# A two-layer encoder on one core: rotary keys as column tiles in the input stage, one product for both meta values, and a new order on TensorE

## The chip, the cores and the metric

The kernel runs on one core of one Trainium2 chip. The metric is the device time of the whole program in microseconds (us), lower is better. TensorE (PE) multiplies matrices into the banks of PSUM; VectorE (DVE), ScalarE (ACT) and GpSimd (POOL) work element by element; SyncE (SP) issues transfers (DMA).

## What is computed

Two request groups, one of 256 tokens and one of 512, each with 16 meta tokens ahead, pass through the same two layers, in float32. 272 + 528 = 800 tokens in all. Cut to what matters:

```python
for i in range(2):
    mix = mla_mixer(h, ...) if i == 0 else gqa_mixer(h, ...)
    h = layer_norm(DN_ALPHA * h + mix, ln1_g[i], ln1_b[i])
    h = layer_norm(DN_ALPHA * h + sqrelu_mlp(h, w1, w2), ln2_g[i], ln2_b[i])
return h[:, N_META:]

def mla_mixer(x, ...):                       # dense attention, 16 heads
    c = x @ w_in                             # 1024 -> 768 (q) + 256 (kv) + 32 (rotary key)
    cq, ckv = rms_norm(c[..., :768], g_q), rms_norm(c[..., 768:1024], g_kv)
    kr = apply_rope(c[..., 1024:], cos, sin) # one rotary key for all heads
    q = cq @ w_uq                            # per head 64 plain + 32 rotated
    kn, v = split(ckv @ w_ukv)
    s = qn @ kn + qr @ kr                    # softmax(s / sqrt(96)) @ v, then @ w_o

def gqa_mixer(x, ...):                       # window of 128, 16 query heads, 4 key heads, sinks
    q, k, v = split(x @ w_qkv)               # meta tokens are seen by every block

def sqrelu_mlp(x, w1, w2):
    h = relu(x @ w1)
    return (h * h) @ w2
```

## The kernel before

Activations lie with features on the 128 partitions and tokens along the free axis, in halves of 400 columns. For accuracy every large product is three products of fp32r operands: an operand is split into a rounded high part and the remainder, and `mm3` adds high x high, high x low and low x high in one bank (lines 510, 511 and 512 of the profile). The splits cost one ACT cast and one DVE subtraction each.

*Input stage.* `c = x @ w_in` is computed in columns of 128 features, in the order `IN_ORDER = [6, 7, 8, 0, 1, 2, 3]`, and columns 4 and 5 at the end by `pair`, which saves products by sums of blocks (a Strassen-like scheme). Columns 6 and 7 are ckv, column 8 is the rotary key, repeated four times to fill 128 features, columns 0 to 5 are cq. Weights of the first three columns and the eight slices of x come in quarters and slices from SP's queue; PE works through three columns as slices land. `post` evicts a column: for column 8 four DVE operations make the rotated key `kr` from two tables; for others it stores the column and adds its squares up on DVE. After column 8 `key_norm` takes the root of the mean of squares of ckv: `rstd_bcast` splits the sums, lets PE add them over partitions and broadcast them in one go, and takes Sqrt on ACT and the reciprocal on DVE over 128 x 400 elements. `sums(k)` makes the block sums for `pair` from x, for which slices are loaded again (`load_again`) save those kept in their buffers (`KEPT`).

*Planned stages.* From attention on, each stage is a list of tasks given to `Plan.task` with engine, cost in ns, what it reads and writes. `Plan.order` simulates the stage by these costs and writes the instructions down in the order of their simulated begins. The order on PE isn't left to it: `ORDERS` holds a permutation of PE's tasks for each of four stages (attention of layer 0, its MLP, attention of layer 1, its MLP). Costs decide the order on the other engines, and for tasks given by `either` whether POOL or DVE does them (the weight sums of the MLP's Strassen-like products, for instance, line 1502). `Plan.lag` is the time from the end of a task to the start of one that waits for it.

*Attention of layer 0.* Scores go to two banks `sa`; a group of scores is one chunk of queries for one pair of heads or one head. DVE takes the negative maximum (line 1124), ACT the exponential (line 1128 or 1138), then a reciprocal and a scaling, PE transposes the probabilities (`wa<-ident,p`, line 1186) and multiplies them with the values as fp32 products in two column tiles of 64 (`wa<-pt,v`, line 1219). An fp32 product shows as two records.

*Attention of layer 1.* `values` computes v in blocks of 128 tokens, and apart from them the 16 meta tokens of each group as a product of 16 rows.

Of the kernel before, what the change touches and what calls it, by code (L numbers as in the profile page):

```python
# [47 lines left out]
IN_ORDER = [6, 7, 8, 0, 1, 2, 3]  # L48
# [3 lines left out]
KEPT = (3,)  # L52
# [78 lines left out]
]  # L131


LEAD = (1400, 3000, 1400, 0)


class Held:


    def __init__(self, tag, make, t=None):  # L140
        self.tag, self.make, self.t, self.left, self.fresh, self.after = tag, make, t, 0, True, ()


class Plan:

    LAG = {"PE": 190, "DVE": 70, "ACT": 70, "POOL": 90, "SP": 0}

    last, count = {}, 0

    def __init__(self, bufs, own, in_turn=()):
        self.bufs, self.own, self.tasks, self.last, self.ways = bufs, own, [], {}, []
        self.no, Plan.count = Plan.count, Plan.count + 1
# [2510 lines left out]
```

## Time and profile before

| | |
|---|---|
| median of 3 runs | 1743.28 us (1742.0 to 1743.66) |
| the profiled execution | 1743.47 us, span 1741.6 us |
| granted clock of TensorE, mean | 0.998 |
| PE busy | 1726.0 us, 99% of the span, 10806 records |
| DVE busy | 1432.8 us, 82% |
| ACT busy | 1027.5 us, 59% |
| POOL busy | 335.4 us, 19% |
| DMA | 124.15 MB, mean 71 GB/s |

Busy times are from records; records of one engine overlap their neighbours, so a share near 100% doesn't yet say that no time is left between two instructions. The distance from start to start tells more.

### The profile page before, as it was taken

What the parts mean: (1) busy time and instruction counts of PE and PEld (TensorE: products, weight loads), DVE (VectorE), ACT (ScalarE), POOL (GpSimd) and SP (SyncE); (2) the same over time, 40 slices, a digit from 0 to 9 for tenths busy, and PEclk for the clock granted to TensorE, in tenths of its full rate; (3) what the DMA queues carried; (4) which work ended last, traced back from release to release, by engine and by line L of the source; (5) the groups of instructions that cost most, each with busy time, mean ns of one, the idle gap of its engine ahead of it and who ended that gap; (6) DMA issues with size and microseconds to landing.
All of it is one profiled execution on the core that took longest, in us unless ns stands there. A gap on an engine that the chain in (4) does not pass through costs nothing.

```text
span 1741.6 us, 28738 instructions
## 1 busy us (share of the span) xinstructions
PE 1726.0 (99%) x10806; PEld 1628.5 (94%) x10806; DVE 1432.8 (82%) x2921; ACT 1027.5 (59%) x2172; POOL 335.4 (19%) x306
## 2 busy tenths in 40 slices
PE   9999999999999999999999999999999999999998
PEld 9999999989999999999999998889989889988996
DVE  7888888887877899888886887876877889889877
ACT  6577777774755446445644627775665455545652
POOL 0011111112210111111202223332201133322200
PEclk9999999999999999999999999999999999999999
DMA  7201001014311221122122221012311222222222
GB/s 253 78 32 32 20 23 54 23 42 164 99 61 49 73 67 67 61 85 73 52 75 99 88 85 57 26 50 76 106 61 49 73 74 73 73 73 73 73 68 90
DMA packets 39451, 124.15 MB, mean 71 GB/s; under 512 B 4752, under 2 KB 9744, under 8 KB 39184
## 3 DMA queue, kind: packets, MB, share of 16 engines
q1 hardware_dynamic: 39312, 122.31, 21.2%
q8 instruction: 85, 1.39, 0.3%
q14 instruction: 54, 0.44, 0.1%
HBM read 119.15 MB, written 3.15 MB: 70 GB/s over the span
## 4 chain that ended last, share of the span: by engine, by line
PE 97%; DVE 2%; ACT 1%; issue 0%; DVEq 0%; POOL 0%; ACTq 0%; POOLq 0%
PE w L510 18%; PE w L511 18%; PE w L512 18%; PE wb L510 4%; PE wb L511 4%; PE wb L512 4%; PE wa L510 3%; PE wa L512 3%; PE wa L511 3%; PE wa L1219 2%; PE sa L510 2%; PE wa L1186 2%; PE sa L512 2%; PE sa L511 2%; PE wb L2373 2%; PE wb L2355 2%
## 5 line engine op out<-in xcount | busy, mean ns | idle before, releaser
L1798 DVE TENSOR_TENSOR acc<-acc,w 128x400 f32<-128x400 f32 (+1 forms) x306 | 183.5, 620 | 53.7 <-PE w L512 51.4
L510 PE MATMUL w<-h,wspi 128*128 128x400 f32 x320 | 110.2, 344 | 0.8 <-DVE acc L1305 0.8
L511 PE MATMUL w<-h,wspi 128*128 128x400 f32 x320 | 110.3, 345 | 0.0
L512 PE MATMUL w<-h,wspi 128*128 128x400 f32 x320 | 110.2, 344 | 0.0
L510 PE MATMUL w<-h,wsp 128*128 128x400 f32 x312 | 108.0, 346 | 0.4 <-DVE acc L1798 0.4
L511 PE MATMUL w<-h,wsp 128*128 128x400 f32 x312 | 107.7, 345 | 0.2 <-DVE h L1530 0.2
L512 PE MATMUL w<-h,wsp 128*128 128x400 f32 x312 | 107.3, 344 | 0.0
L1530 DVE TENSOR_TENSOR h<-sq,h 128x400 fp32r<-128x400 f32 (+1 forms) x167 | 102.2, 628 | 3.5 <-ACT h L1528 3.3
L1528 ACT CAST h<-sq 128x400 fp32r<-128x400 f32 (+1 forms) x167 | 84.3, 518 | 19.9 <-DVE sq L1536 10.9
L1155 POOL TENSOR_TENSOR p<-p,rs 106x512 f32<-106x512 f32 (+1 forms) x40 | 45.0, 1126 | 251.4 <-DVE pk L1146 117.6
L1128 ACT ACTIVATE p<-sa,nm,rq 106x528 f32<-106x528 f32 (+1 forms) x80 | 63.5, 794 | 17.0 <-DVE nm L1125 12.6
L1709 ACT COPY sq<-w 128x400 f32<-128x400 f32 (+1 forms) x69 | 33.6, 487 | 67.7 <-PE w L512 67.0
L1124 DVE TENSOR_REDUCE nm<-sa 106x1 f32<-106x528 f32 (+1 forms) x80 | 56.2, 704 | 16.2 <-PE sa L512 14.7
L510 PE MATMUL w<-wsp,h 128*128 128x512 f32 (+1 forms) x176 | 69.5, 395 | 0.0
L512 PE MATMUL w<-wsp,h 128*128 128x512 f32 (+1 forms) x176 | 69.2, 393 | 0.0
L512 PE MATMUL w<-wspi,h 128*128 128x512 f32 (+1 forms) x176 | 69.1, 393 | 0.0
L510 PE MATMUL w<-wspi,h 128*128 128x512 f32 (+1 forms) x176 | 69.1, 392 | 0.0
L511 PE MATMUL w<-wspi,h 128*128 128x512 f32 (+1 forms) x176 | 69.1, 392 | 0.0
L511 PE MATMUL w<-wsp,h 128*128 128x512 f32 (+1 forms) x176 | 69.1, 392 | 0.0
L510 PE MATMUL sa<-k,q 128*106 128x264 f32 (+5 forms) x208 | 64.0, 308 | 2.9 <-ACT p L1138 2.9
L510 PE MATMUL w<-t,wspi 128*128 128x400 f32 (+1 forms) x180 | 61.5, 342 | 0.0
L512 PE MATMUL w<-t,wspi 128*128 128x400 f32 (+1 forms) x180 | 61.5, 342 | 0.0
(824 smaller groups left out, 6173.1 us busy)
## 6 DMA issues: line engine op xcount, KB each, us to landing
wrawo<-in_w_o_dram SPq DMA_DIRECT2D x32, 512.0 KB, 3.3
wraw0d<-in_w2b_dram SPq DMA_DIRECT2D x24, 512.0 KB, 3.3
wraw1d<-in_w2b_dram SPq DMA_DIRECT2D x18, 512.0 KB, 3.5
wrawq<-in_w_q_dram SPq DMA_DIRECT2D x8, 512.0 KB, 3.3
xr<-in_xT_dram SPq DMA_DIRECT2D x16, 200.0 KB, 3.1
wraw<-in_w_qn_dram SPq DMA_DIRECT2D x8, 384.0 KB, 3.0
wx1d<-in_w2b_dram SPq DMA_DIRECT2D x6, 512.0 KB, 3.3
out_dram<-fo SPq DMA_DIRECT2D x11, 256.0 KB, 2.0
```

What stands on the lines that cost most here:

```text
L510: nc.tensor.matmul(out, lh, rh, start=start, stop=False, **kw)
L511: nc.tensor.matmul(out, lh, rl, start=False, stop=False, **kw)
L512: nc.tensor.matmul(out, ll, rh, start=False, stop=stop, **kw)
L1124: plan.task("DVE", DVE(528), lambda: V.tensor_reduce(nm.t[:qm, 0:1], v(), axis=AX.XY, op=ALU.max, negate=True), reads=[ps], writes=[nm], n ...
L1128: lambda: S.activation(P_().rearrange("p (a b) -> p a b", b=264), v(), AF.Exp, bias=nm.t[:qm, 0:1], scale=sc, accum_out=rs.t[:qm, 0:1]),
L1155: f = lambda row=row, r=r, w=w: G.tensor_tensor(row()[:, META:T], row()[:, META:T], r().to_broadcast([qm, w]), ALU.mult)
L1186: nc.tensor.transpose(ps.t[:, k * qm : (k + 1) * qm], src[k], ident[:qm, :qm])
L1219: nc.tensor.matmul(av[64 * e : 64 * e + 64, :n], vt.t[:, k, h0 + 64 * e : h0 + 64 * e + 64], PT.t[:, e, k, :n], start=k == 0, stop=False, ...
L1528: plan.task("ACT", 530, lambda: S.copy(d.t[:, 0], c.t[:, :n]), reads=[c], writes=[(d, "hi")], new=[d])
L1530: "DVE", 570, lambda: V.tensor_tensor(d.t[:, 1], c.t[:, :n], d.t.bitcast(F32)[:, 0], ALU.subtract),
L1798: f = lambda: V.tensor_tensor(z, z, ps.t[:, : z.shape[-1]], ALU.add)
L2355: nc.tensor.transpose(ps.t[:, n * P : (n + 1) * P], SM.t[:, a : a + P], ident)
```

## The change

*Input stage.* Column 8 is dropped from `IN_ORDER`. The rotary key is computed from the raw x slices and a 32-feature weight `wkr` as plain fp32 products in four column tiles of 32: tile i takes tokens 200 i to 200 i + 199, so that the result lies 32 partitions for each quarter of the tokens. `key_rotate` rotates it in half-width operations, and `kr` is kept split already. `key_norm` now adds squares over partitions with the squares as weights against a column of ones (`ks`), takes root and reciprocal on 100 x 8 elements, and broadcasts by products with the identity (`rs`). The squares' sums of columns 1, 2, 3 and 7 move from DVE to POOL. The first quarters of the second and third weight column and `wkr` are issued on ACT's queue ahead of its table load. Four slices of x are kept rather than two (`KEPT`), and `sums` stands earlier.

*Keys in attention.* The key's copies into the attention's buffers are plain copies on ACT and DVE, ten each, instead of six casts and six subtractions.

*Meta values in layer 1.* POOL copies (`meta_along`) line up the meta columns of both groups, and one product of 48 rows replaces the two of 16.

*Planner.* Lags depend on both engines; an engine is free again before its task's cost is over (`OVER`: DVE 82, ACT 100, POOL 30 ns); PE tasks have kinds (F ordinary, T transposes and the like, C column tiles, R row tiles), and `CHANGE` adds a cost where the kind changes; costs of PE and POOL tasks are new (a POOL sum of weights 1296 or 1620 ns instead of 1040). All four rows of `ORDERS` are new.

```diff
-IN_ORDER = [6, 7, 8, 0, 1, 2, 3]
+IN_ORDER = [6, 7, 0, 1, 2, 3]
+KR = NT // 4
-KEPT = (3,)
+KEPT = (2, 3)
...
-    "0 4 3 1 6 5 2 8-9 7 11-12 10 13-15 18 21 20 17 22 24-25 16 23 19 27 26 29 28 30 32-33 31 35 37 34 36 38-44 46-49 52 50-51 53 55 45"
...
-    LAG = {"PE": 190, "DVE": 70, "ACT": 70, "POOL": 90, "SP": 0}
+    LAG = {"PE": 198, "DVE": 45, "ACT": 45, "POOL": 50, "SP": 0}
+    CHANGE = {
+        "TF": 85, "CF": 85, "RF": 105, "FC": 100, "FR": 105, "FT": 5, "TT": 65, "TC": 165, "TR": 177,
+        "CT": 50, "RT": 60, "CR": 15, "RC": 5, "FF": 0, "CC": 0, "RR": 0,
+    }
+    OVER = {"PE": 0, "DVE": 82, "ACT": 100, "POOL": 30, "SP": 0}
...
+        a, b = self.tasks[i][0], self.tasks[k][0]
+        if a == "PE" or a == "SP":
+            return 0 if a == b or a == "SP" else 198
+        return {"PE": 90, "POOL": 78}.get(b, 34)
+
+    def hold(self, e, cost):
+        return cost / 2 if e == "SP" else max(cost - self.OVER[e], cost / 2)
...
+            e, cost, run = tasks[b][:3]
+            cost += self.CHANGE[self.kinds[a] + self.kinds[b]]
...
+    wkr = gp.tile([P, 8, 32], F32, tag="wkr", name="wkr")
+    slices[0][0](nc.sync, False)
+    slices[1][0](nc.scalar, False)
+    nc.scalar.dma_start(wkr, ins["w_kr"])
+    slices[2][0](nc.scalar, False)
...
+        def key_rope(k, xr, c):
+            for i in range(c.start // KR, c.stop // KR):
+                nc.tensor.matmul(
+                    pkr[32 * i : 32 * i + 32], wkr[:, k], xr[:, i * KR : (i + 1) * KR],
+                    start=k == 0, stop=k == 7, tile_position=(0, 32 * i), skip_group_check=True,
+                )
...
-                V.tensor_tensor(place["ssq"][:, c] if o == 5 else t, t, sq, ALU.add)
+                (V if o in (4, 5) else G).tensor_tensor(place["ssq"][:, c] if o == 5 else t, t, sq, ALU.add)
...
+        def key_norm():
+            ks = ps_l("ks")
+            for i in range(8):
+                nc.tensor.matmul(ks[:100, i : i + 1], sums_of[1, i // 4][:, i % 4 * 100 : (i % 4 + 1) * 100], ones, start=True, stop=True)
+            rk = gp.tile([P, 8], F32, tag="rk", name="rk")
+            S.activation(rk[:100], ks[:100, :8], AF.Sqrt, bias=eps_rms[:100], scale=1.0 / 256)
+            V.reciprocal(rk[:100], rk[:100])
...
+                for i in range(4):
+                    nc.tensor.matmul(rs[:, i * 100 : (i + 1) * 100], rk[:100, 4 * h + i : 4 * h + i + 1].to_broadcast([100, P]), ident[:100, :100], start=True, stop=True)
...
-    DVE, ACT, POOL = lambda n: 150 + 1.05 * n, lambda n: 170 + 0.835 * n, lambda n: 185 + 1.67 * n
+    DVE, ACT, POOL = lambda n: 150 + 1.05 * n, lambda n: 170 + 0.835 * n, lambda n: 185 + 2.17 * n
...
+            plan.task("POOL", 1620 if slow else POOL(w), lambda: f(G), other=("DVE", DVE(w), lambda: f(V)), **kw)
...
-            for kind, i, a in [(("m", 0, 0), ("b", 0, 16), ("b", 1, 144), ("b", 2, 272)), (("b", 3, 0), ("m", 1, 128), ("b", 4, 144), ("b", 5, 272))][hf]:
+            for kind, i, a in [(("b", 0, 16), ("b", 1, 144), ("b", 2, 272)), (("m", 0, HALF), ("b", 3, 0), ("b", 4, 144), ("b", 5, 272))][hf]:
...
-                m = META if kind == "m" else P
+                m = 3 * META if kind == "m" else P
```

What this does to the order of instructions, at three places.

PE at the program's start. `in` are the banks of the input columns, `x` the split activations, `wsp` split weights, `pkr` the bank of the rotary keys. Before, after the warm-up products:

```order
L548 MATMUL warm<-part 128x128 x7
L510 MATMUL in_217<-x_123,wsp_126 128x400
L510 MATMUL in_245<-x_123,wsp_126 128x400
L511 MATMUL in_217<-x_124,wsp_126 128x400
L512 MATMUL in_217<-x_123,wsp_126 128x400
L510 MATMUL in_278<-x_123,wsp_128 128x400
L511 MATMUL in_278<-x_124,wsp_128 128x400
L510 MATMUL in_307<-x_123,wsp_128 128x400
L510 MATMUL in_341<-x_123,wsp_130 128x400
L511 MATMUL in_341<-x_124,wsp_130 128x400
```

The same place now:

```order
L572 MATMUL warm<-part 128x128 x7
L603 MATMUL pkr<-xr_139,wkr 32x200 x4
L545 MATMUL in_255<-x_134,wsp_61 128x400
L546 MATMUL in_255<-x_135,wsp_61 128x400
L547 MATMUL in_255<-x_134,wsp_61 128x400
L545 MATMUL in_283<-x_134,wsp_61 128x400
L545 MATMUL in_316<-x_134,wsp_63 128x400
L546 MATMUL in_316<-x_135,wsp_63 128x400
L545 MATMUL in_345<-x_134,wsp_63 128x400
L603 MATMUL pkr<-xr_156,wkr 32x200 x2
```

The key products of the first slice stand ahead of all columns and wait for raw x alone, those of each later slice stand among the columns' products; `in_341`, then column 8, is gone, and the third weight column is column 0.

PE at the start of attention of layer 0, around the fourth and fifth group of scores (two banks `sa`, taken in turn). Before:

```order
L512 MATMUL sa_1166<-k_915,q_908 106x264
L510 MATMUL sa_1166<-k_915,q_907 106x264
L511 MATMUL sa_1166<-k_916,q_907 106x264
L512 MATMUL sa_1166<-k_915,q_908 106x264
L510 MATMUL sa_1116<-k_917,q_909 106x264
L511 MATMUL sa_1116<-k_918,q_909 106x264
L512 MATMUL sa_1116<-k_917,q_910 106x264
```

The same place now:

```order
L546 MATMUL wa_929<-cq_128,wspi_687 128x264
L547 MATMUL wa_929<-cq_127,wspi_687 128x264
L545 MATMUL wa_929<-cq_127,wspi_687 128x264
L546 MATMUL wa_929<-cq_128,wspi_687 128x264
L547 MATMUL wa_929<-cq_127,wspi_687 128x264
L1234 MATMUL wa_912<-ident,p_1140 128x92 x4
L545 MATMUL sa_1100<-k_895,q_887 106x264
L546 MATMUL sa_1100<-k_896,q_887 106x264
L547 MATMUL sa_1100<-k_895,q_888 106x264
```

Before, the fifth group (`sa_1116`, k_917) follows the fourth at once; now 18 products of queries, of which the last are shown, and a transposed chunk stand ahead of the fifth (`sa_1100`).

PE in the values of layer 1 (`hb` are the activations of the half, `q` the buffer in which the meta columns are lined up). Before, the first rows of one of the two meta products, of 24 rows each:

```order
L510 MATMUL wb_9657<-wspi_709,hb_9545 16x256
L511 MATMUL wb_9657<-wspi_709,hb_9545 16x256
L512 MATMUL wb_9657<-wspi_709,hb_9546 16x256
L510 MATMUL wb_9657<-wspi_709,hb_9545 16x256
L511 MATMUL wb_9657<-wspi_709,hb_9545 16x256
```

Now, the first rows of the only one:

```order
L545 MATMUL wb_9571<-wspi_724,q_1_9956 48x256
L546 MATMUL wb_9571<-wspi_724,q_1_9956 48x256
L547 MATMUL wb_9571<-wspi_724,q_1_9956 48x256
L545 MATMUL wb_9571<-wspi_724,q_1_9956 48x256
L546 MATMUL wb_9571<-wspi_724,q_1_9956 48x256
```

Twenty-four products of the first kind are gone; the other twenty-four have 48 rows.

More of the change, by code (lines that the diff above doesn't have):

```diff
@@ L174, in held, with task @@
         return h
-    def task(self, engine, cost, run, reads=(), writes=(), new=(), port=False, ends=(), other=None):
+    def task(self, engine, cost, run, reads=(), writes=(), new=(), port=False, ends=(), other=None, kind="F"):
         n, deps, held = len(self.tasks), set(), {}
@@ L395, in load, with part @@
         raw = self.pool.tile([P, 1024], F32, tag="wraw", name=f"wraw{i}", bufs=self.raw_bufs)
-        def part(a, b):
-            nc.sync.dma_start(raw[:, a:b], src[:, a:b])
+        def part(a, b, queue=None, split=True):
+            if queue is not None:
+                queue.dma_start(raw[:, a:b], src[:, a:b])
+            if not split:
+                return
             nc.scalar.copy(sp[:, 0, a:b], raw[:, a:b])
             nc.vector.tensor_tensor(sp[:, 1, a:b], raw[:, a:b], sp.bitcast(F32)[:, 0, a:b], ALU.subtract)
-        self.parts = [lambda a=a: part(a, a + n // parts) for a in range(0, n, n // parts)]
+        self.parts = [lambda queue=nc.sync, split=True, a=a: part(a, a + n // parts, queue, split) for a in range(0, n, n // parts)]
         if parts == 1:
@@ L474, in ps_s, with use @@
         return bank("s", name, (P, 2, 512))
+    specs = []
+    def use(key, src, n=1024, where=None):
+        specs.append((key, src, n, where))
+    for o in IN_ORDER:
+        use(("in", o), ins["w_in"][o])
+    use(("qr", 0), ins["w_qr"][0], 768, "late")
+    use(("kv", 0), ins["w_kv"][0], 1024, "late")
+    for key in [("up", j) for j in UP_FIRST[:2]] + [("dn", 7, i) for i in range(3)] + [("up", j) for j in UP_FIRST[:2]]:
+        use(key, None, where="given")
+    W = Weights(nc, wp, specs, WRAW, NWSP, NWSP - 1)
+    slices = []
+    for _ in range(3):
+        W.load(4)
+        slices.append(W.parts)
+    wkr = gp.tile([P, 8, 32], F32, tag="wkr", name="wkr")
[3 more added lines that the diff above has]
+    slices[2][0](nc.scalar, False)
     ident = gp.tile([P, P], F32, tag="ident", name="ident")
@@ L527, in split @@
         return S.copy(hi, src).ins, V.tensor_tensor(lo, src, hi.bitcast(F32), ALU.subtract).ins
-    def rstd_bcast(tp, sums, n, count, eps, nm):
-        d = tp.tile([P, 2, HALF], F32R, tag="xr", name=f"hl{nm}", bufs=XR)
-        split(d[:, 0, :n], d[:, 1, :n], sums)
-        out = ps_l(f"rb{nm}")[:, :n]
-        for x in range(2):
-            nc.tensor.matmul(out, partr, d[:, x, :n], start=x == 0, stop=x == 1)
-        S.activation(out, out, AF.Sqrt, bias=eps, scale=D / count)
-        V.reciprocal(out, out)
-        return out
     def sq_tile(pool, nm):
@@ L572, in tile_encoder @@
         x = [xp.tile([P, 8, NT], F32R, tag=f"x{i}", name=f"x{i}") for i in range(2)]
-        table = xp.tile([P, 2, NT], F32, tag="table", name="table", bufs=1)
-        cos0, sin0 = table[:, 0], table[:, 1]
+        craw = xp.tile([P, 2, NT], F32, tag="craw", name="craw")
+        table = xp.tile([P, 2, KR], F32, tag="kt", name="kt", bufs=1)
+        pkr = ps_l("pkr")[:, :KR]
         again = {}
-        slices = []
-        for _ in range(3):
-            W.load(4)
-            slices.append(W.parts)
+        def key_rope(k, xr, c):
[4 more added lines that the diff above has]
+                )
         for k in range(8):
@@ L626, in sums @@
             b12, b11, b22, b21 = up[:, :HALF], up[:, HALF:], low[:, :HALF], low[:, HALF:]
+            rest[k] = b21, b22
             V.tensor_tensor(b11, b12, b11, ALU.subtract)
@@ L767, in tile_encoder @@
                 post(o, h, ps[:, :HALF])
-                if o == 8 and h == 1:
-                    key_norm(0)
-                    key_norm(1)
-                if o == 8 and h == 1:
-                    w22 = xp.tile([P, 2 * NT], F32R, tag="table", name="w22i", bufs=1)
-                    TS[2].append([xp.tile([P, HALF], F32R, tag="ksh", name=f"tk{i}", bufs=2) for i in range(2)])
-                    TS[2].append([w22[:, 1024:1424], xp.tile([P, HALF], F32R, tag="tk", name="tk")])
-                    w22 = w22[:, :1024].rearrange("p (a b) -> p a b", a=2)
-                if o in (0, 1):
-                    k = 2 * o + h
-                    load_again(k)
-                    sums(k)
+                if o == 7 and h == 1:
+                    for k in KEPT:
+                        sums(k)
+                    key_rotate()
+                    key_norm()
+                    for k in KEPT:
+                        put_by(k)
+                    for k in (0, 1):
+                        load_again(k)
+                if o == 0:
+                    sums(h)
+                    put_by(h)
                 if o == 2 and h == 0:
@@ L840, in mean @@
             def mean():
-                plan.task("PE", 690, lambda: nc.tensor.matmul(pm.t[:, :n], part, ss(), start=True, stop=True), reads=[("ss", hf), *st], writes=[pm], new=[pm], ends=ends)
+                plan.task("PE", 365, lambda: nc.tensor.matmul(pm.t[:, :n], part, ss(), start=True, stop=True), reads=[("ss", hf), *st], writes=[pm], new=[pm], ends=ends)
                 for o in range(8):
@@ L859, in run @@
                         nc.tensor.matmul(sb.t[:g, i : i + 1], v.t[:, i * g : (i + 1) * g], ones, start=True, stop=True)
-                plan.task("PE", 700, run, reads=[v], writes=[sb], new=[sb], ends=ends)
+                plan.task("PE", 645, run, kind="T", reads=[v], writes=[sb], new=[sb], ends=ends)
                 m = n // g
@@ L1186, in run @@
                         nc.tensor.transpose(ps.t[:, k * qm : (k + 1) * qm], src[k], ident[:qm, :qm])
-                plan.task("PE", 4 * 0.9 * qm, run, reads=[(pt, x) for x in range(len(es))], writes=[ps], new=[ps])
+                plan.task("PE", 48 + 2.38 * qm, run, kind="T", reads=[(pt, x) for x in range(len(es))], writes=[ps], new=[ps])
                 def copy():
@@ L1203, in run @@
                         nc.tensor.transpose(ps.t[:, e * qx : (e + 1) * qx], pk[e][:qx], ident[:qx, :qx])
-                plan.task("PE", 200, run, reads=[("pk", no % 3, e, j) for e in range(2) for j in range(3)], writes=[ps], new=[ps])
+                plan.task("PE", 120, run, kind="T", reads=[("pk", no % 3, e, j) for e in range(2) for j in range(3)], writes=[ps], new=[ps])
                 plan.task(
@@ L1671, in run @@
                             nc.tensor.transpose(ps.t[:, o * P : (o + 1) * P], acc[:, hf, 4 * q + o, a : a + P], ident)
-                    plan.task("PE", 460, run, reads=[("acc", hf, 4 * q + o) for o in range(4)], writes=[ps], new=[ps])
+                    plan.task("PE", 354, run, kind="T", reads=[("acc", hf, 4 * q + o) for o in range(4)], writes=[ps], new=[ps])
                 for i, (t, x) in enumerate([(0, 0), (1, 0)] if q == 0 else [(2, 0), (0, 1), (1, 1), (2, 1)]):
@@ L1828, in part @@
                     reads = [*wparts(w, slice(512 * ps[0], 512 * (ps[-1] + 1))), *[(ops[p][x], y) for p in ps for y in ("hi", "lo")]]
-                    plan.task("PE", 3 * len(ps) * (MM if l == 0 else 227), run, reads=reads, writes=[banks[q]], new=[banks[q]] if start and ps[0] == 0 else [])
+                    plan.task("PE", 3 * len(ps) * (MM if l == 0 else 233), run, reads=reads, writes=[banks[q]], new=[banks[q]] if start and ps[0] == 0 else [])
                     if ps[-1] == len(ops) - 1:
```

170 lines of the change are left out of this document (91 added, 79 removed), and 79 rows, old and new, of the table ORDERS.

## The prediction

> **What bounds the kernel now.** I read the page first (busy shares, the chain that ended last), then who TensorE (PE) waited for, longest first.
>
> ```profile
> span 1741.6 us, 28738 instructions
> PE 1726.0 (99%) x10806; PEld 1628.5 (94%) x10806; DVE 1432.8 (82%) x2921; ACT 1027.5 (59%) x2172; POOL 335.4 (19%) x306
> PE 97%; DVE 2%; ACT 1%; issue 0%; DVEq 0%; POOL 0%; ACTq 0%; POOLq 0%
> ```
> ```profile
> PE sa L510 <- ACT p L1138: 2.9, 2, 2.4
> PE warm L548 <- POOL part L482: 1.1, 1, 1.1
> PE w L510 <- DVE acc L1305: 0.8, 1, 0.8
> PE wb L2355 <- DVE sma L2330: 0.6, 1, 0.6
> PE wb L869 <- DVE rstb L864: 0.6, 1, 0.6
> PE inx L510 <- ACT in L740: 0.6, 1, 0.6
> PE w L510 <- DVE acc L1798: 0.4, 1, 0.4
> PE w L511 <- DVE h L1530: 0.2, 1, 0.2
> PE w L1571 <- DVE sqsum L2413: 0.2, 1, 0.2
> ```
>
> PE is the chain from end to end, and all its listed waits add to 7.4 us. So the time is PE's own instructions: what matters is how many the change removes or adds, at what distance from start to start (a record's duration overlaps the next one's and is no price). The stalls are a second, small pot.
>
> **Price of an ordinary product.** The first window below is input stage alone, 400 columns wide; its columns are each engine's busy time and, in brackets, instructions.
>
> ```profile
> 12.00:60.00 48.00, 48.00 (x265) 48.00 (x264) 42.36 (x70) 28.97 (x54) 0.00 (x0) 1.00 0.53 186
> 973.60:976.20 2.60, 2.60 (x24) 2.13 (x23) 2.19 (x5) 1.05 (x2) 1.26 (x2) 1.00 0.08 20
> ```
>
> Two of the 265 overlap the edges, so 48/263 = 0.1825 us each, at granted clock 1.00. The second window holds the 24 products of 16 rows x 256 columns of one of the two GQA meta values: 2.60/23 = 0.113 us each.
>
> **Removed from PE.** The ninth input column (rotary keys) is 8 slices x 3 products x 2 halves = 48 x 0.1825 = -8.76 us. The two key-norm broadcasts lose 4 fp32r products of the same width: -0.73. One meta value product of 48 rows replaces two of 16; the distance of those rows is that of 256 columns, not of rows, so 24 vanish: 24 x 0.113 = -2.71. Sum -12.2.
>
> **Added to PE: the rotary keys.** 32 fp32 products of 200 columns by 32 array columns. No trace row has four column tiles side by side; the nearest are two tiles of 64.
>
> ```profile
> 146.44 0.29 PE L512 MATMUL wa<-cq,wspi 128*128 128x272 f32 x1
> 146.66 1.64 PE L1219 MATMUL wa<-pt,v 128*64 128x210 f32 x16
> 148.13 0.53 PE L1227 MATMUL wa<-ptm,vm 128*64 128x106 f32 x8
> ```
>
> An fp32 product leaves two records, so x16 is 8 products in 4 pairs, started in 148.13 - 146.66 = 1.47 us: 0.37 for a pair of 210 columns, 0.35 for 200. (One alone I take at the same 0.35, an estimate: nothing in these rows shows one tile slowing the other.) Going into column tiles took 146.66 - 146.44 = 0.22 where the 272-column neighbours are 0.125 apart: a switch is 0.095, and I take the same for the way out. The order issues the keys in 9 groups (slice 1 in two halves): if the four tiles overlap as the two do, 9 x 0.35 + 18 x 0.095 = +4.9. Bounds: 16 pairs one after the other, 5.6 + 1.7 = +7.3; no overlap at all, 32 x 0.35 + 1.7 = +12.9; below, slices 0 and 1 sink in the waits of the first microseconds (next rows), 6 x 0.35 + 12 x 0.095 = +3.2. I take 4.9, nearest to the pair row, which shows tiles side by side.
>
> The Trainium skill, "TensorE: Matmul & The Clock Gate", section "Measured speedup vs the span model", gives 3.07x for four row tiles and says column tiles come close; "TensorEngine Tiling (Array Packing)", section "Key Properties", says that a change of tiling mode drains the engine. By 3.07 the keys would be 32 x 0.35/3.07 + 1.7 = 5.4, an estimate from that page, and the sum 0.5 us less; the drain, the rule that speaks against the change, is in the trace at 0.095 us, so it does not sink it.
>
> ```profile
> 4.40 1.42 PE L510 MATMUL in<-x,wsp 128*128 128x400 f32 x2
> 5.95 0.54 PE L512 MATMUL in<-x,wsp 128*128 128x400 f32 x1
> 6.28 0.54 PE L510 MATMUL in<-x,wsp 128*128 128x400 f32 x1
> 3.29 0.41 ACT L399 CAST wsp<-wraw 128x256 fp32r<-128x256 f32 x1 [1.07 <-DMA wraw<-in_w_in_dram]
> 2.11 0.91 SPq L398 DMA_DIRECT2D wraw<-in_w_in_dram  x2
> ```
>
> PE is short of data from 4.40 and still at 0.33 a product at 6.28. The two weight quarters and the small key weight now issue on ScalarE's (ACT's) queue: at SP's 0.45 each, 1.36 us ahead of its table load and first cast, which idled 1.07: up to 0.3 late, while SP's x slices issue 0.9 earlier. I count zero. The reload of an x buffer now also waits for PE's key products; they stand early, and three columns of weights are PE's backlog.
>
> **Added to PE: the key norm.** It sums by 8 fp32 products against ones and broadcasts by 8 against the identity, twice what one layer norm does:
>
> ```profile
> 431.63 0.78 PE L859 MATMUL wa<-ones,sqa 128*100 128x1 f32 x8
> 433.46 1.03 PE L869 MATMUL wa<-ident,rsta 100*128 100x100 f32 x8
> ```
>
> Less the last record's drain these are 0.65 and 0.87 us, so 2 x 1.52 = +3.0. Their wait: squares, a POOL sum, ones, Sqrt on ACT, reciprocal on DVE, then the broadcast, with 40 products (7.3 us) ahead of the first and 29 (5.3 us) between the two on PE's queue. A late link stalls everything behind; I count zero because DVE is relieved here:
>
> ```profile
> 0.00:105.00 105.00, 103.35 (x615) 102.21 (x616) 87.03 (x166) 68.13 (x141) 9.10 (x28) 1.00 0.42 143
> L537 DVE RECIPROCAL rbkv<-rbkv 128x400 f32<-128x400 f32 x2 | 5.3, 2664 | 1.5 <-ACT rbkv L536 1.5
> L706 DVE TENSOR_TENSOR ss<-ss,sq 128x400 f32<-128x400 f32 x7 | 4.0, 583 | 0.0
> L687 DVE STREAM_SHUFFLE ksh<-in 128x400 f32<-128x400 f32 x2 | 1.2, 620 | 0.0
> ```
>
> Gone from DVE: 5.3 of reciprocals, four key operations twice (4.7 at about 0.58), two splits (1.2), and 8 sums of squares handed to POOL (4.7), which did nothing from 12 to 60 us. Against this stand five half-width operations and four more key copies: some 12 us less, for a stage about 7 us shorter. If DVE still ran behind, what stands ahead of the reciprocal in its queue after the column's eviction would be late with it: four to five operations of about 0.6, some 3 us, the bound.
>
> **Order.** Counted in the two programs, switches into, out of and between column- and row-tiled products fall from 117 to 120 - 18 (the keys' own) = 102: 15 x 0.1 = -1.5. The one large stall is at the start of attention:
>
> ```profile
> 105.71 0.28 PE L511 MATMUL sa<-k,q 96*106 96x264 f32 x1
> 105.83 0.28 PE L512 MATMUL sa<-k,q 96*106 96x264 f32 x1
> 107.16 0.57 ACT L1138 ACTIVATE p<-sa,nm,rq 90x272 f32<-90x272 f32 x1
> 108.48 0.34 PE L510 MATMUL sa<-k,q 128*106 128x264 f32 x1 [2.37 <-ACT p L1138]
> ```
>
> The fifth group of scores needs the bank of the third, whose exponentials run at 107.16. Now 18 products of queries and 4 transposes stand between the fourth and the fifth (18 x 0.122, the distance of the 264-wide rows, and some 0.3: 2.5 us): I take -2.0, between 0 and -2.4. What is late next there is DVE's maximum of the scores. The other waits after the start add to 3.4 us; a searched order may take them or set new ones: 0, with -3.4 and +4 as ends.
>
> **POOL's work in the MLP stages.** The planner's new POOL prices hand about 80 sums of weights to DVE:
>
> ```profile
> L1502 POOL TENSOR_TENSOR wraw1d<-wraw1d,wraw1d 128x512 f32<-128x512 f32 x14 | 22.8, 1631 | 70.4 <-DVE wsp L1491 30.7 <-ACT h L1528 12.4 <-ACT w L1485 10.0
> L1502 DVE TENSOR_TENSOR wraw0d<-wraw0d,wraw0d 128x512 f32<-128x512 f32 x31 | 23.0, 762 | 4.8 <-DMA wraw0d<-in_w2b_dram 4.8
> 455.00:930.00 475.00, 474.32 (x2602) 473.23 (x2603) 400.31 (x641) 257.84 (x463) 68.99 (x52) 1.00 0.21 70
> 1250.00:1700.00 450.00, 450.00 (x2297) 408.53 (x2295) 373.76 (x565) 251.28 (x460) 96.63 (x71) 1.00 0.22 71
> L1798 DVE TENSOR_TENSOR acc<-acc,w 128x512 f32<-128x512 f32 x138 | 92.7, 684 | 35.3 <-PE w L512 34.0
> ```
>
> 80 x 0.76 = 61 us on DVE over 925, from 84% to 90%. Its idle time in these stages is mostly waiting for PE, so this costs nothing as long as DVE stays ahead.
>
> **Tail.** In the order one BN_STATS fewer stands behind the last product; 3 take 1.07 us there:
>
> ```profile
> 1734.16 1.07 DVE L1980 BATCH_NORM_STATS2 fm<-acc 128x6 f32<-128x256 f32 x3
> ```
>
> -0.35. The rest is hidden: fewer rotary table bytes and one weight less to read (DMA was half used in 12 to 60), the POOL copies that line up the meta columns, and four more small key copies on ACT.
>
> **Sum.** -12.2 + 4.9 + 3.0 - 1.5 - 2.0 - 0.35 = -8.1 us. The profiled execution took 1743.47 (span 1741.6), 0.2 above the median of the runs, 1743.28. So 1735.2 beside that median.
>
> **Rivals.**
> - *The gain is eaten in the input stage: no change.* The four tiles do not overlap (12.9, not 4.9: +8.0), or they run as pairs (+2.4) and the norm's broadcast is late (+3). For it: no row shows four tiles, and DVE was 88% busy in 12 to 60 us. Against: the pair row overlaps fully. It gives 1740.6 to 1743.2. Chance 0.17.
> - *DVE becomes the bound in the MLP stages: slower.* PE holds its banks until DVE has accumulated them (L1798). Of the 61 us, whatever falls on stretches where DVE has no slack comes back as PE waits. It turns slower when more than 8.1 + 3.5 = 11.6 us do, a fifth of them; a third would be 20 us, so 1755. For it: 90% as a mean leaves stretches near 100%. Against: PE's longest wait for accumulation is 0.8 today, and DVE's records overlap each other, so 90% is less than it looks. Chance 0.07.
> - *The order takes all stalls as well.* -8.1 - 0.4 - 3.4 = -11.9: 1731.4. For it: the listed waits are few and single. Against: PE already waits in only nine places. Chance 0.14.
>
> **How the numbers follow.** My forecast has 0.62: 1735.2, own range 1732 to 1739.5. Two runs of this kernel can be told apart from about 0.2%, 3.5 us, so faster means below 1739.8 and slower above 1746.8. Forecast and third rival make faster 0.76; the first rival, mostly, same 0.17; the second slower 0.07. The range reaches down into the third rival and up to the first's end: 1730.5 to 1743.
>
> **What would show it.** Right: 10826 PE records (-48 - 4 - 24 + 64 + 32, the last two being fp32), 20 more in less time; groups of x8 at the keys' line that start 0.35 us apart, four tiles at nearly one time; no wait over 1 us at the broadcast or at the fifth score; DVE near 90% in the MLP stages, with PE still full. Wrong: key tiles one after another; a PE wait on DVE's reciprocal near 45 us; waits for accumulation that add to several us between 450 and 1700. Most of all I would be wrong if the sums moved to DVE delayed its bank releases.

## The result and the profile after

The changed kernel takes 1750.08 us (median of 5 runs, 1749.7 to 1752.11) against 1743.28: slower by 6.8 us, ratio 1.0042 with an interval of 1.0027 to 1.0056. The profiled execution took 1749.82. 1735.2 was predicted. The head of the page, and its chain by engine:

```profile
span 1748.0 us, 28663 instructions
PE 1723.0 (99%) x10826; PEld 1619.4 (93%) x10826; DVE 1444.6 (83%) x3001; ACT 1019.6 (58%) x2173; POOL 220.4 (13%) x226
PE 87%; DVE 8%; ACT 4%; issue 1%; DMA 0%; POOL 0%; SPq 0%; DVEq 0%; ACTq 0%; POOLq 0%
```

PE has the 10826 records that the prediction counted and is busy 3 us less, yet the span is 6.4 us longer. The chain, 97% PE before, now runs through DVE and ACT for 12% of the span. Who PE waited for, the longest of 21 lines (9 before; us in total, times, longest):

```profile
PE sa L545 <- ACT p L1186: 3.1, 4, 1.5
PE wb L2408 <- ACT vm L2300: 1.6, 1, 1.6
PE sa L547 <- DVE q L859: 1.6, 2, 1.0
PE sa L545 <- ACT p L1176: 1.1, 4, 0.5
...
PE wa L1234 <- DVE k L859: 0.8, 1, 0.8
...
PE wa L1251 <- DVE q L859: 0.7, 1, 0.7
```

`sa` and `wa` are layer 0's attention, `wb` layer 1's. To see where the time went, the span is cut at PE's first product of a stage (the first `wa`, `w`, `wb`, the last `wb`, the last product). The last measured column is e3, a kernel told of below: the change without its new planning of layer 0's attention.

| stage, us | before | after | predicted | e3 |
|---|---|---|---|---|
| input | 84.0 | 83.5 | -1.6 | 83.7 |
| attention, layer 0 | 371.0 | 378.9 | -3.5 with all switches | 369.8 |
| MLP, layer 0 | 472.2 | 471.5 | 0 | 471.5 |
| attention, layer 1 | 314.9 | 314.9 | -2.7 | 313.7 |
| MLP, layer 1 | 491.4 | 491.5 | 0 | 491.5 |
| behind PE's last product begins | 8.1 | 7.7 | -0.35 | 7.7 |

One stage carries the loss, layer 0's attention. (Layer 1's takes 1.2 more than in e3, since PE ran at half clock behind its wait of 1.6, `wb`; the last section tells of that.) What changed in layer 0's attention shows on the engines that feed PE. First DVE's and ACT's waits in that stage before, then after:

```profile
DVE nm L1124 <- PE sa L512: 14.7, 31, 1.4
...
DVE rs L1131 <- ACT p L1128: 2.2, 6, 0.5
...
ACT p L1128 <- DVE nm L1125: 12.6, 18, 1.9
...
ACT p L1138 <- DVE nm L1134: 3.1, 6, 1.0
```
```profile
DVE rs L1179 <- ACT p L1176: 20.1, 32, 1.5
...
DVE nm L1172 <- PE sa L547: 5.5, 5, 1.9
...
ACT p L1176 <- DVE nm L1173: 23.3, 27, 1.9
ACT p L1186 <- DVE nm L1182: 15.3, 11, 2.8
```

Before, DVE stood ready at the maximum (`nm`) and waited for PE's scores: it was ahead. After, it stands at the reciprocal (`rs`) and waits for the exponential (`p`), ACT waits for DVE's next maximum, and PE for both. It looks as if DVE's and ACT's queues held their work in an order that does not fit the times it takes; the experiments test that.

### The profile page after: what moved, and what is told of

It is laid out like the page before. It is cut to its first block, busy times and chain, and to the rows that moved or that the text cites. A ratio compares the mean times of both kernels' runs of the same rounds, so it can differ in the third digit from the quotient of the medians.

```text
span 1748.0 us, 28663 instructions
## 1 busy us (share of the span) xinstructions
PE 1723.0 (99%) x10826; PEld 1619.4 (93%) x10826; DVE 1444.6 (83%) x3001; ACT 1019.6 (58%) x2173; POOL 220.4 (13%) x226
## 4 chain that ended last, share of the span: by engine, by line
PE 87%; DVE 8%; ACT 4%; issue 1%; DMA 0%; POOL 0%; SPq 0%; DVEq 0%; ACTq 0%; POOLq 0%
PE w L546 18%; PE w L545 18%; PE w L547 18%; PE wb L545 4%; PE wb L546 4%; PE wb L547 4%; PE wa L545 2%; PE wa L547 2%; PE wa L546 2%; PE wa L1267 1%; PE wb L2434 1%; PE wb L2416 1%; PE wa L1234 1%; PE sa L545 1%; PE wb L2338 1%; PE sa L547 1%
## 5 line engine op out<-in xcount | busy, mean ns | idle before, releaser
L545 PE MATMUL w<-h,wsp 128*128 128x400 f32 x324 | 111.7, 345 | 0.0
L546 PE MATMUL w<-h,wsp 128*128 128x400 f32 x324 | 111.7, 345 | 0.0
L547 PE MATMUL w<-h,wsp 128*128 128x400 f32 x324 | 111.4, 344 | 0.0
L546 PE MATMUL w<-h,wspi 128*128 128x400 f32 x308 | 106.2, 345 | 0.0
L547 PE MATMUL w<-h,wspi 128*128 128x400 f32 x308 | 105.9, 344 | 0.0
L545 PE MATMUL w<-h,wspi 128*128 128x400 f32 x308 | 105.9, 344 | 0.0
L1578 DVE TENSOR_TENSOR h<-sq,h 128x384 fp32r<-128x384 f32 (+1 forms) x164 | 92.8, 576 | 8.3 <-ACT h L1576 6.8
L1576 ACT CAST h<-sq 128x384 fp32r<-128x384 f32 (+1 forms) x164 | 82.3, 518 | 23.6 <-DVE sq L1584 13.0
L545 PE MATMUL w<-wspi,h 128*128 128x512 f32 (+1 forms) x190 | 74.4, 392 | 0.0
L547 PE MATMUL w<-wspi,h 128*128 128x512 f32 (+1 forms) x190 | 74.2, 390 | 0.0
L546 PE MATMUL w<-wspi,h 128*128 128x512 f32 (+1 forms) x190 | 74.1, 390 | 0.0
L545 PE MATMUL w<-wsp,h 128*128 128x512 f32 x162 | 64.1, 395 | 0.0
L546 PE MATMUL w<-wsp,h 128*128 128x512 f32 x162 | 64.0, 395 | 0.0
L547 PE MATMUL w<-wsp,h 128*128 128x512 f32 x162 | 64.0, 395 | 0.0
L546 PE MATMUL w<-t,wsp 128*128 128x384 f32 (+1 forms) x184 | 62.6, 340 | 0.0
L547 PE MATMUL w<-t,wsp 128*128 128x384 f32 (+1 forms) x184 | 62.6, 340 | 0.0
L545 PE MATMUL w<-t,wsp 128*128 128x384 f32 (+1 forms) x184 | 62.5, 340 | 0.0
```

Source lines behind the costliest of these rows:

```text
L545: nc.tensor.matmul(out, lh, rh, start=start, stop=False, **kw)
L546: nc.tensor.matmul(out, lh, rl, start=False, stop=False, **kw)
L547: nc.tensor.matmul(out, ll, rh, start=False, stop=stop, **kw)
L1576: plan.task("ACT", 530, lambda: S.copy(d.t[:, 0], c.t[:, :n]), reads=[c], writes=[(d, "hi")], new=[d])
L1578: "DVE", 570, lambda: V.tensor_tensor(d.t[:, 1], c.t[:, :n], d.t.bitcast(F32)[:, 0], ALU.subtract),
```

## The experiments

All kernels differ from the changed one only where said; each has its median and its ratio to the kernel before. `a0` is layer 0's attention. "Old" is what the kernel before has.

**Order or prices?** A two by two in a0: PE's order (`ORDERS[0]`), and the planner's numbers (lags, `OVER`, `CHANGE`, costs).

```diff
 ORDERS = [
-    "0-2 4 3 6 5 8 7 9-12 ...",          # e1, e3, e4: the old row
+    "0 4 3 1 6 5 2 8-9 7 11-12 ...",
...
+        if self.no in OLDP:               # e2, e3: {0}; e4: {0, 2}; the same for lags, CHANGE, costs
+            return cost / 2 if e == "SP" else cost
         return cost / 2 if e == "SP" else max(cost - self.OVER[e], cost / 2)
```

> The changed kernel with the PE order of layer 0's attention (only that one of the four) set back to the old one; the planner's new constants still set the order of the other engines there. The stage took 371.0 us before and 378.9 after. Theory T1 (the new constants give DVE, ACT and POOL an order that their real times do not keep; PE then waits): the waits stay, stage 376 to 380, kernel 1748 to 1751. Theory T2 (the new PE order itself asks for results too early): stage 370 to 372, kernel 1741.5 to 1743.5. Theory T3 (DVE starts the stage late because of the input stage and the 20 narrow key copies): no recovery, 1749 to 1751.

> The changed kernel with the planner's old lags, costs, overlaps and no price for a change of tiling in layer 0's attention; PE keeps the new order there. T1: most of the 7.9 us comes back, stage 371 to 374, kernel 1742 to 1745. T2: nothing comes back, stage 377 to 382, kernel 1748 to 1753. T3: nothing comes back either, 1749 to 1751.

> The changed kernel with both the old constants and the old PE order in layer 0's attention; input stage, MLP stages and the second attention stay new. T1 and T2: the stage is as before, 370 to 372, kernel 1741.5 to 1743.5. T3: the stage stays at 377 to 379 since the late start is still there, kernel 1748 to 1751. This run parts T3 from the other two.

> As the run before, and the old constants and the old PE order (without the dropped meta value product) in layer 1's attention too. If the order or the constants ate the 2.7 us of the meta product there, the stage from the first wb product to the last goes from 314.9 to about 312, and the kernel to 1738.5 to 1740.5, below the kernel before. If the meta product gains nothing by itself (its eight ACT copies or the lined-up columns are late), the stage stays at 314 to 315 and the kernel within 0.5 us of the run before.

| a0, us (kernel, ratio) | old PE order | new PE order |
|---|---|---|
| old numbers | e3: 369.8 (1739.58, 0.9985 [0.9976, 0.9994]) | e2: 375.0 (1746.2, 1.0017 [1.0008, 1.0025]) |
| new numbers | e1: 388.1 (1760.06, 1.0101 [1.0087, 1.0115]) | after: 378.9 (1750.08, 1.0042) |

T3 falls: with the new input stage kept, e3 has no loss (it even lies below the 370 to 372 of T1 and T2). T1 holds in its direction: the new numbers cost 3.9 us with the new order and 18.3 with the old (e1 holds, like the kernel before, some 1.6 us that a stretch at half clock adds, told of at the end). T2 holds in part: the new order costs 5.2 with the old numbers, but brings 9.2 with the new ones. The two depend on each other, which neither theory said: e1 lies far above T1's 376 to 380, and e2 between the ranges of T1 and T2. DVE's first wait in a0 of e1 and of e3 shows the same two pictures as after and before:

```profile
DVE rs L1141 <- ACT p L1138: 24.3, 37, 1.5
```
```profile
DVE nm L1145 <- PE sa L520: 14.6, 30, 1.2
```

e4 has 314.6 in layer 1's attention, 0.95 more than e3, and 1740.42 (0.9989 [0.9981, 0.9998]): there the new order and numbers do no harm.

**Which number?** The exponential first, since its trace shows a part that the new cost of 795 ns leaves out: a second record that reads the accumulated sum.

```profile
145.29 0.79 ACT L1176 ACTIVATE p<-sa,nm,rq 106x528 f32<-106x528 f32 x1 [1.39 <-DVE nm L1173]
145.98 0.19 ACT L1176 ACTIVATION_READ_ACCUMULATOR p<-sa,nm,rq 106x1 f32 x1
146.10 0.79 ACT L1176 ACTIVATE p<-sa,nm,rq 106x528 f32<-106x528 f32 x1
```

```diff
-                    "ACT", 795,      # and 578 -> 660
+                    "ACT", 880,
```

> The changed kernel with one pair of numbers set back: the planner's costs of the two exponentials in layer 0's attention, 880 and 660 ns again instead of 795 and 578. The trace shows each as two records, ACTIVATE (0.79 or 0.57 us) and, starting 0.1 before its end, ACTIVATION_READ_ACCUMULATOR of 0.19, which gives the sum free: 0.88 and 0.66 together. Theory T1a (the planner leaves out this second record, puts the reciprocal 85 ns too early into DVE's queue, and DVE and ACT then wait for each other): most of the 7.9 us comes back, stage 367 to 372, kernel 1738 to 1743. Theory T1b (the overlap of neighbouring records that the planner assumes) and T1c (the shorter lags): little comes back, stage 376 to 379, kernel 1747 to 1750.

> The same two costs set back, with the old PE order in layer 0's attention, where the new constants took the stage from 369.8 to 388.1. T1a: most of the 18.3 us comes back, stage 370 to 374, kernel 1739.5 to 1744. T1b or T1c: stage 383 to 388, kernel 1754 to 1760. A part in between would say that the exponentials are one cause of two.

> The changed kernel (new PE order, exponentials at 795 and 578) with the assumed overlap taken out of the planner for layer 0's attention alone: each instruction holds its engine for its whole cost. T1b: stage 368 to 373, kernel 1739 to 1744. T1a: the reciprocal still comes too early; ACT is given 0.1 more for each task by this, which hides some of it: stage 374 to 379, kernel 1745 to 1750.

> The changed kernel with only the old lags between engines (70 ns after DVE and ACT, 90 after POOL, 190 after PE) in the planner for layer 0's attention. T1c: stage 368 to 373, kernel 1739 to 1744. T1a: 36 ns more on each step from ACT to DVE stand in for two fifths of the missing 85: stage 374 to 378, kernel 1745 to 1749. T1b: no change, 378 to 379, 1749 to 1751.

> Old PE order in layer 0's attention, new lags, costs and prices of tiling changes, but no assumed overlap there. With all new constants this order took 388.1 us for the stage, with all old ones 369.8. Theory T1b (the assumed overlap is what makes the planner's order of DVE and ACT fail): stage 369 to 373, kernel 1739 to 1743.5. A theory that needs several constants together: 376 to 384, kernel 1746 to 1754.

e7 and e9 change one line for a0 (e8 the lags alone in the same way):

```diff
+        if self.no == 0:
+            return cost / 2 if e == "SP" else cost
         return cost / 2 if e == "SP" else max(cost - self.OVER[e], cost / 2)
```

| | a0, us | kernel, ratio |
|---|---|---|
| e5 exponentials | 380.2 | 1749.46, 1.0040 [1.0028, 1.0053] |
| e6 exponentials, old order | 384.8 | 1757.11, 1.0080 [1.0066, 1.0094] |
| e7 no overlap | 375.7 | 1746.73, 1.0022 [1.0013, 1.0031] |
| e8 lags | 378.9 | 1750.01, 1.0042 [1.0029, 1.0054] |
| e9 no overlap, old order | 370.9 | 1743.65, 1.0004 [0.9995, 1.0013] |

T1a, my first guess, falls: the missing record is real, but its price brings nothing in e5 and 3.3 of 18.3 us in e6. T1c falls. T1b holds for what the numbers cost: without the overlap 1.1 us is left of their loss with the old order (370.9 beside 369.8) and 0.7 of the 3.9 with the new one. e7 alone would not tell: its 375.7 lies in the range given for T1a, which e5 rules out, and above that of T1b, because the order's own 5.2 remain. Both edits take the overlap from DVE, ACT and POOL at once, so how much of this is DVE's was not separated.

**Why is the overlap wrong here?** DVE's queue in the changed kernel (start, duration):

```profile
105.01 0.43 DVE L859 TENSOR_TENSOR k<-wa,k 64x264 fp32r<-64x264 f32 x1
105.46 0.42 DVE L1032 CAST q<-y 32x528 fp32r<-32x528 f32 x1
105.91 0.43 DVE L859 TENSOR_TENSOR q<-wa,q 64x264 fp32r<-64x264 f32 x1
...
106.95 0.33 DVE L1200 TENSOR_SCALAR p<-p,rs 92x256 f32<-92x256 f32 x1
107.22 0.71 DVE L1181 TENSOR_REDUCE nm<-sa 90x2 f32<-90x544 f32 x1
107.85 0.33 DVE L1200 TENSOR_SCALAR p<-p,rs 92x256 f32<-92x256 f32 x1
```

The lower three start 0.06 to 0.08 us before the one ahead ends, as `OVER` assumes (82 ns). The upper three do not: each starts 0.01 to 0.03 after it. They are the halves of `q` and `k` on 64 rows and copies of 32 rows, at changing first rows. The Trainium skill, "VectorE: DVE Perf Modes", section "Two Vector instructions with no wait between them", has a rule for this: an instruction whose input or output starts in another group of 32 partitions than the last one in that memory starts only when all earlier ones have finished. Applied to the program's DVE instructions of a0, 858 successions, it holds back 221 of those that did not wait longer, and all 221 stand apart, by 0.01 to 0.04. Of the 538 others 453 overlap, 22 a little, and 63 stand apart (43 of these read what the one ahead wrote). So the trace agrees. The number of rows does not sort them so: 68 successions with an instruction of 64 or 32 rows overlap, and none of these is held back. In layer 1's attention the rule holds back none, and 492 of 551 overlap: there `OVER` is a right price. In a0 some 221 x 0.11 = 24 us of DVE's time are missing from the plan (0.08 of assumed overlap and 0.03 of gap each).

Two kernels let only instructions of more than 64 rows overlap in a0's plan, one takes the overlap out of layer 1's attention:

```diff
-            free[e] = t + self.hold(e, cost)
+            full[e] = t + cost + 25 * (e in ("DVE", "ACT"))      # a narrow one starts at full[e], a wide one at free[e]
+            free[e] = full[e] if self.narrow[i] else t + self.hold(e, cost)
```

> The changed kernel with its new PE order and all its new constants, but in layer 0's attention the planner assumes the overlap of 82 (DVE) and 100 ns (ACT) only between instructions of more than 64 rows, and 25 ns of gap around those of 32 or 64 rows. In the trace of the changed kernel's attention 375 of 552 successions of wide DVE instructions overlap, of those with a narrow one 67 of 293 (199 stand 0.01 to 0.03 apart: 21.7 us that the planner does not count). Theory T1d (this missing time is what goes wrong): at least as good as no overlap at all (375.7): stage 370 to 375.7, kernel 1741 to 1746.5. If the wide ones are at fault too (dependent steps, semaphores): 377 to 379, kernel 1748 to 1750.

> The same planner, with the exponentials at 880 and 660 ns as well, and the old PE order. T1d: stage 369 to 372, kernel 1738.5 to 1742. If not: 376 to 386, kernel 1746 to 1756.

> The kernel with old constants and old PE order in layer 0's attention (1739.6), with the assumed overlap taken out in layer 1's attention too, where PE order and all else stay new (stage 313.7; its PE waits are 1.6, 0.9, 0.7, 0.6 and 0.3). If the assumed overlap costs there what it does in layer 0: stage 311 to 312.7, kernel 1737 to 1738.7, the best yet. If not: 313.3 to 315, kernel 1739 to 1741, and the part of the meta product's gain that is missing lies in PE's order there.

e10: a0 376.3, kernel 1747.65 (1.0023 [1.0014, 1.0032]), about as near as e7. e11: 377.1, again with a stretch at half clock, kernel 1746.98 (1.0026 [1.0016, 1.0037]). The narrow instructions' price, with the exponentials', thus brings 11.0 us beside e1 (388.1, the same stretch in both), but e9 without any overlap is some 4.6 better still. Both missed the range of T1d, e10 by 0.6 us and e11 by 5. What else the plan gets wrong there stays open; 24 of the 221 held successions have no narrow instruction, and these two kernels let them overlap, as they do the dependent steps. e15: layer 1's attention takes 316.4 against 313.7, kernel 1744.09 (1.0006 [0.9997, 1.0015]). My expectation was wrong, and the result fits the rule: where the overlap is real, leaving it out of the plan costs 2.7 us. (The kernel is 4.5 above e3; in the profiled execution the other 1.9 lie in the input stage, which the edit does not touch.) A rival remains, that any number other than those on which an order was searched disturbs the plan, right or wrong. Against it speaks that the new order too is better without the overlap, 375.7 against 378.9.

**Is caution free?** Old numbers, but each DVE instruction 60 ns longer:

```diff
-            return cost / 2 if e == "SP" else cost
+            return cost / 2 if e == "SP" else cost + (60 if e == "DVE" else 0)
```

> Old constants and old PE order in layer 0's attention (stage 369.8, kernel 1739.6), and the planner made pessimistic there: each DVE instruction holds the engine 60 ns longer than its cost. If an error on this side is free (an engine that is ahead of its plan waits, and PE does not): stage 369 to 371, kernel 1739 to 1741. If the planner has to be right on both sides: stage 373 or more, kernel above 1743.

> The same pessimistic planner with old constants, but with the new PE order, which took 375.0 with old constants and 375.7 with no overlap. Theory T2a (the 5 to 6 us that the new PE order costs beside the old one come from DVE being late even so): stage 371 to 374, kernel 1742 to 1745. Theory T2b (PE's own order asks for results sooner than the chain through DVE, ACT and POOL can give them, whatever those do first): stage 374.5 to 377, kernel 1745.5 to 1748.

No: a0 takes 386.8 in e13 and 404.7 in e14, kernels 1758.06 (1.0086 [1.0072, 1.0099]) and 1776.59 (1.0192 [1.0178, 1.0206]). Stretches at half clock, 6.8 us in e13 and 17 in e14, account for at most half their length of this, 3.4 and 8.5. In e13 DVE is ahead and waits for scores, as in the kernel before but for longer, and PE waits for exponentials all the same:

```profile
DVE nm L1145 <- PE sa L520: 26.8, 35, 2.4
```
```profile
PE sa L518 <- ACT p L1159: 5.5, 4, 2.4
```

e14 went the wrong way, so it decides nothing between T2a and T2b.

**Is another order bad in itself?** PE's order in a0 was searched again. Each order was judged by running the planned queues with the durations, overlaps and gaps that the traces show.

```diff
 ORDERS = [
-    "0 4 3 1 6 5 2 8-9 7 11-12 ...",
+    (a row of its own)                    # e16: no overlap in the plan; e17, e18: the old numbers
```

> Layer 0's attention planned with no assumed overlap, the other new constants kept, and a PE order of its own: searched again from the old order, judged by how late PE ends when the planned queues are run with the durations, overlaps and gaps that the traces show (an overlap only between instructions of more than 64 rows). All else as in the changed kernel. Theory T4 (the order and the prices have to be searched together, on prices that the chip keeps; the changed kernel's order was fitted to prices that it does not keep): better than both the old order with the same constants (370.9) and the old pair (369.8), whose listed PE waits are 2.7 us: stage 366 to 369, kernel 1735.5 to 1739. Rival (the stage is at what the chain through DVE and ACT allows, and any other order is worse): 371 to 376, kernel 1741 to 1746.

> The same search, from the new order and with the planner's old constants in layer 0's attention. T4: the stage falls from the 375.0 of the new order with these constants to 366 to 369, kernel 1735.5 to 1739: the order's 5 us were a misfit to the constants, and nothing that the order's distances force. Rival: 372 to 376, kernel 1742 to 1746.

> The old constants in layer 0's attention, as in the best kernel so far (1739.6, stage 369.8), and a PE order searched again from the old one on durations and overlaps that the traces bear out, now judged by the end of every engine's queue and not by PE's alone: the run on the search without that took 366.1 us for the stage, but left DVE and ACT with 7 to 10 us of the next stage's input, which then started late and at half clock. T4: stage 365.5 to 368, the MLP stage behind it 471 to 472, kernel 1735 to 1738, the best of all. Rival (what the order saves comes back at the border of the stages or in new waits): kernel 1739 to 1745.

e16's a0 takes 366.1, the shortest of all, with PE busy from edge to edge (first row below). But the search looked at PE's end alone, and DVE and ACT carried the stage's last work over the border: the MLP's stage behind it takes 483.5 instead of 471.5, kernel 1750.16 (1.0035 [1.0022, 1.0048]).

```profile
84.00:451.00 367.00, 366.09 (x3049) 343.62 (x3049) 302.83 (x863) 261.98 (x657) 59.25 (x58) 1.00 0.17 52
451.00:465.00 14.00, 4.57 (x16) 3.24 (x15) 10.18 (x15) 2.96 (x8) 8.31 (x6) 0.74 0.24 76
```
```profile
PE w L1590 <- DVE sqsum L1331: 7.0, 1, 7.0
PE w L517 <- DVE h L830: 2.4, 1, 2.4
```

e17 fails the same way (377.4 with a wait of 6.1 at the border; 1750.87, 1.0039 [1.0026, 1.0052]). e18, judged by all queues' ends, has 471.1 behind the border and 1739.93 (1738.3 to 1742.77; 0.9982 [0.9973, 0.9991]); its profiled a0 of 371.5 holds a wait of 1.5 at its start and 6.8 us at half clock behind it, as e17's does:

```profile
86.50:93.30 6.80, 6.80 (x32) 6.80 (x33) 4.18 (x11) 2.93 (x13) 1.49 (x3) 0.50 0.25 77
```

So T4 holds in part: an order searched on durations that the traces show costs nothing beside the old pair, where the changed kernel's order costs 5 with the same numbers. It does not beat the old pair; without the stretch at half clock its a0 would take some 368, an estimate (371.5 less half of 6.8). That the changed kernel's order is slow because it was searched on wrong prices is likely by this, but not shown: no run here shows how that order was found.

**The meta product.** Eight ACT copies read the 48-row product out of its bank. In e3 three ran, then a table load and four exponentials, then five, and PE waited 1.6 us for the bank. e12 puts the product ahead of three groups of scores.

```diff
-... 88 89 92 90 91 97 93 ...             # 91 is the meta product
+... 88 91 89 92 90 97 93 ...
```

> The kernel with old constants and old PE order in layer 0's attention (1739.6), and in layer 1's attention the meta value product moved ahead of three groups of scores in PE's order. There PE waits 1.6 us for a bank that the product fills and eight small ACT copies read out: three of them ran, then a table load and four exponentials (4.3 us), then the other five. Ahead of those, the copies end before the table load: the wait of 1.6 goes, the stage from 313.7 to 312.0 to 312.4, kernel 1738 to 1738.5. Rival: the copies are still spread, or another bank is late: 313.2 to 314.5, kernel 1739 to 1740.5.

The rival was right: the stage takes 313.67 as in e3, and PE waits 1.9 on the transposes' other input instead:

```profile
PE wb L2381 <- DVE pk L2352: 1.9, 1, 1.9
```

The kernel takes 1739.58 (0.9984 [0.9975, 0.9993]). With e3 it is the fastest: 3.7 us below the kernel before, 10.5 below the changed one.

## Why the prediction was wrong

The step that failed is the last of "Order": "a searched order may take them or set new ones: 0, with -3.4 and +4 as ends". With the two terms beside it (-1.5 and -2.0) the order was to bring 3.5 us. e3 has all of the change but a0's order and numbers; from e3 to the changed kernel it is 1739.58 to 1750.08, 10.5 more. By the profiled executions 9.1 of it lie in that stage, far over the +4, and 1.2 in layer 1's attention (the half clock). I read the planner's numbers as what hands POOL's sums to DVE, and never asked whether the new overlap is what DVE's records do in this stage. The trace of before had it: in its a0 the rule above holds back 194 successions that did not wait longer, and all 194 stand apart. The bound of +4 has no source in the prediction, and the -3.4 beside it is the sum of waits that were there; the waits that an order can make do not depend on those. What stays open is why the new order costs 5.2 even with the old numbers.

The rest of the sum, -12.2 + 4.9 + 3.0 - 0.35 = -4.65, is within a microsecond of e3's 3.7 below before. That is in part luck. By stages e3 gains 0.3 in the input, 1.1 in layer 0's attention, 0.6 in its MLP, 1.2 in layer 1's attention and 0.4 at the end, and none of these terms stands for the two of layer 0. (The first is about what the stretch at half clock cost there before, 1.6, which e3 lacks.) The terms, one by one:

- *Input stage*: 0.3 to 0.5 less in e3 and after rather than 1.6, and in five of the later traces 1.3 to 1.6 more than before, since PE came to full speed later (last section). The four tiles do overlap, but a group costs more than 0.54. From the product ahead of it to the second behind it 12.32 to 13.37 is 1.05, less two at 0.1825, so 0.685; and there are ten groups, not nine (slice 0 is halved too), so at most 6.9 - 4.9 = 2.0 more. The stage shows 1.1 of it; two of the groups stand in the waits of the first microseconds.

```profile
12.32 0.34 PE L546 MATMUL in<-x,wsp 128*128 128x400 f32 x1
12.60 0.55 PE L603 MATMUL pkr<-xr,wkr 128*32 128x200 f32 x8
13.08 0.45 PE L546 MATMUL in<-x,wsp 128*128 128x400 f32 x1
13.37 0.35 PE L547 MATMUL in<-x,wsp 128*128 128x400 f32 x1
```

- *Key norm*: no wait at `ks` or `rs` is in the list; counting it at zero was right. So the first rival falls in both its mechanisms, late broadcasts and tiles one after another.
- *Meta product*: 1.2 instead of 2.7; the bank wait of 1.6 took the rest, and e12 shows a second wait of about that size behind it.
- *The stall at 105.8*: it went (0.7 is left around there), as said. But it went in e3 as well, with the old order and numbers: there the fifth group starts without a listed wait and waits 0.9 for `q` at its third product. So the new order was not needed for these 2.0. The third rival, that the order takes all stalls, has the sign wrong.

```profile
106.59 0.34 PE L518 MATMUL sa<-k,q 128*106 128x264 f32 x1
...
107.98 0.37 PE L520 MATMUL sa<-k,q 128*106 128x264 f32 x1 [0.93 <-DVE q L832]
```

- *Switches*: whether 15 fewer bring 1.5 was not measured by itself.
- *Sums on DVE*: DVE's busy share in the two MLP stages is 86 and 87%, 90 was expected, and the stages did not grow. The second rival falls: slower came true, but not by its mechanism.
- *Tail*: 0.4 less; 0.35 was worked out.

```profile
450.00:930.00 480.00, 479.83 (x2638) 478.83 (x2637) 413.12 (x690) 256.02 (x461) 19.05 (x15) 1.00 0.21 70
1250.00:1700.00 450.00, 448.79 (x2293) 407.07 (x2292) 389.95 (x622) 249.90 (x461) 26.09 (x21) 1.00 0.21 70
```

## What to carry to other kernels

A planner's constant is a change to every queue that it orders: check it against successions of records in each stage, by kind, before costing it at nothing, and expect an error of either sign to cost. An order and the numbers of the planner work as a pair: beside the old pair the two mixed ones lost 5 and 18 us here, and the new pair 9, each more than all the arithmetic that the change saved. And judge an order by the end of every queue, since what is saved on one engine can come back at the next border.

## What the hardware did that I had not expected

DVE's overlap of 0.06 to 0.08 us between neighbours is lost when the first row of an input or output moves to another group of 32 (all 221 such successions in a0 after, all 194 before; 0.11 us each).

A wait costs PE more than its length. Behind the wait of 2.37 us in the kernel before, and behind the 1.6 us at the meta product's bank after, PE runs at half clock for some 3.2 us, which costs 1.6 where PE has work throughout (columns as in the windows above; the clock is third from the end):

```profile
109.30:112.50 3.20, 3.20 (x17) 3.20 (x16) 3.12 (x12) 0.88 (x2) 0.20 (x1) 0.50 0.36 123
```
```profile
1063.40:1066.60 3.20, 3.20 (x16) 3.20 (x17) 3.04 (x16) 2.90 (x12) 0.15 (x1) 0.50 0.00 0
```

The same pause at that bank stands in 16 of the traces, and half clock follows in 8: layer 1's attention takes 314.9 to 315.5 us with it and 313.4 to 313.7 without. Behind the pause of 1.5 in e17 and e18 it lasts 6.8 us, and behind one of 2.37 in e9 it does not come. The Trainium skill, "TensorE: Matmul & The Clock Gate", section "Part 1: The HAM clock gate (the "warmup" mystery)", says that the clock halves after an idle window of about 3.4 us, and that the windows run freely. A clock of 0.50, and that it comes only at times, agree with that; the length does not, since pauses of 1.7 to 2.7 us from start to start are enough here.

The start of full speed moves as well. No edit touches the input stage, yet it takes 83.3 to 83.8 us in 14 of the 19 traces that have the new one, and 85.4 to 85.6 in five (e6, e12, e14, e15, e16). In those five the early products stand 0.33 us apart until about 10 us; in the others they stand 0.18 apart from about 7 us on. Here e3, then e12:

```profile
6.66 0.35 PE L519 MATMUL in<-x,wsp 128*128 128x400 f32 x1
6.84 0.34 PE L520 MATMUL in<-x,wsp 128*128 128x400 f32 x1
```
```profile
7.29 0.54 PE L519 MATMUL in<-x,wsp 128*128 128x400 f32 x1
7.62 0.54 PE L520 MATMUL in<-x,wsp 128*128 128x400 f32 x1
```
